# Where the modulation of two adaptive-norm layers is computed: TensorE in the mixers, or VectorE in the feed-forward blocks

## The chip, the cores and the metric

The kernel runs on one core of a Trainium2 chip. The metric is the device time of one execution in microseconds (us); the time before is the median of three runs. A profiled execution of the same kernel gives the rows below.

## The reference, cut to what matters

The program is one block of a first network (a feed-forward block "FFN1", a mixer of dilated attention and an RWKV recurrence, a feed-forward block "FFN2"), then two layers of a second network with two streams of 256 tokens each (`x` and `ctx`), width 1024. Each layer of the second network takes six vectors of width 1024 from a condition vector, for each stream:

```python
cond_x = silu(c); cond_c = silu(c_ctx)[None]
for layer in range(2):
    mod_x = split(cond_x @ w_mod[layer] + b_mod[layer], 6)      # w_mod[layer]: 1024 x 6144
    mod_c = split(cond_c @ w_mod[layer] + b_mod[layer], 6)
    hx = adaln(x, norm1_g, mod_x[0], mod_x[1]); hc = adaln(ctx, norm1_g, mod_c[0], mod_c[1])
    mix_x, mix_c = token_mixing(hx, hc, ...)                     # mix_c only in layer 0
    x = x + mod_x[2] * mix_x
    x = x + mod_x[5] * channel_mix(adaln(x, norm2_g, mod_x[3], mod_x[4]))   # layer 0: FFN, layer 1: 8 experts
    # ctx: the same, in layer 0 only
```

The modulation is thus two products of a matrix of 1024 x 6144 with two vectors. It depends on nothing but `c`, `c_ctx` and the weights. All numbers are float32.

## The kernel before, in words

The stages follow one another: FFN1 (`ffn_block`), the first mixer (`mix1`, with `attn1` and then `rwkv`), FFN2 (`ffn_block`), the mixer of layer 0 (`mix2(0)`), its feed-forward block for both streams (`ffn2_block`), the mixer of layer 1 (`mix2(1)`) and the experts (`moe`). Instructions are written as Python generators. A scheduler then sets a fixed order for each engine's queue; an instruction that is written earlier has the higher priority, and one whose inputs and buffers are free earlier may be placed before it. On the chip each queue is worked off in that order.

Weights come through `wraw` (L113): three buffers of 1 MB, loaded by SyncE's queue. `wsplit` (L137) turns each float32 weight tile into a high and a low part: ScalarE casts (`whi`, L149), VectorE subtracts (`wlo`, L150), into 8 pairs of buffers in FFN1 and FFN2 and 6 in `ffn2_block`. A product is then three matmuls (`mm3`, L160 to L162). In `ffn` (L253) the hidden width of 2816 is taken in two halves; a half has six steps over gate and up columns (L261 to L282), and then two column halves of the down product (L283 to L307). In each gate and up step VectorE also has `hh` and `hlo` (L277, L280).

The modulation is `mod` (L836). A column block of 512 of the 6144 columns takes two loads of 1 MB through `wraw` and eight matmuls (L844). Each has 32 columns of weights, two of which are the condition vectors, and writes one of four groups of 32 partitions of a PSUM tile; ScalarE copies the tile (L847), four transposes (L850) put the columns on partitions, and VectorE sums the four groups and adds the bias (L852, L853), into `modT`. After blocks 3 and 9 the gains `gsT` are made. The twelve blocks of layer 0 are woven into `rwkv` (L800: one step of `mod` after four of `rwkv`), with what is left of them behind it (L801). Blocks 0 to 5 of layer 1 are woven into the attention and mLSTM of `mix2(0)`, blocks 6 to 11 into those of `mix2(1)` (L958), and L962 takes what is left. In all, 24 blocks.

`cond` (L824) makes the columns `cT` of the condition vectors early in FFN1. `ffn2_block` makes the rows of its gates (`gate_rows`, 32 matmuls at L169) ahead of its `ffn` loop.

Of the kernel before, what the change touches and what calls it, by code (L numbers as in the profile page):

```python
# [9 lines left out]
F32 = mybir.dt.float32  # L10
# [3 lines left out]
OP = mybir.AluOpType  # L14
AX = mybir.AxisListType
# [4 lines left out]
KT = 8  # L20
# [9 lines left out]
def kview(w, r0, nk, c0, n):  # L30
    return w[r0:r0 + nk * 128, c0:c0 + n].rearrange("(k p) f -> p k f", p=128)


class Builder:
# [295 lines left out]
        nc.vector.scalar_tensor_tensor(y, y, rstd, grow, op0=OP.mult, op1=OP.mult)  # L330
        nc.vector.tensor_tensor(h, y, h, op=OP.add)

    def ffn_block(self, h, pre, wg, wu, wd, post, early=None):
        nc = self.nc
        with self.phase("fp", 8, gu=2, ps=6) as fp:
            x = self.norm_rows_T(fp, h, pre, 2)
            late = True
            for r in self.ffn([x], self.I[wg], self.I[wu], self.I[wd], fp):
                if late:
                    late = False  # L340
                    early()
                    grow = self.row(fp, post, 2)
                    y = self.row_tiles()
                if r is not None:
                    hf, c, t, p = r
                    yv = y[t][:, c * 512:(c + 1) * 512]
                    if hf == 0:
                        nc.scalar.copy(yv, p)
                    else:
                        nc.vector.tensor_tensor(yv, p, yv, op=OP.add)  # L350
                        if c == 1:
                            self.add_post(h[:, t], y[t], grow, 0.5)
                yield
# [482 lines left out]
    def mod(self, L, cbs=range(12), tag="md"):  # L836
        nc = self.nc
        w = self.I["w_mod_2"][L]
        for cb in cbs:
# [19 lines left out]
                                        .to_broadcast([128, KT, 2]), op=OP.mult)  # L859
            yield  # L860

    def ada_T(self, h, L, n, gi, tag="ps"):
        return self.norm_T(h, lambda k: self.gsT[:, L, n, k, gi:gi + 1],
                           lambda k: self.modT[:, L, 24 * n + k, gi:gi + 1], tag)
# [350 lines left out]
    def ffn2_block(self, early):  # L1215
        nc = self.nc
        with self.phase("fp", 6, gu=2, ps=6) as fp:
            xs = [self.ada_T(self.hx, 0, 1, 0), self.ada_T(self.hc, 0, 1, 1)]
            gr = [self.gate_rows(fp, 0, 40, g, "gr%d" % g) for g in range(2)]
            for r in self.ffn(xs, self.I["ffn_w1_2"], self.I["ffn_w3_2"], self.I["ffn_w2_2"], fp):  # L1220
                if r is not None:
                    hf, c, t, p = r
                    self.gated_add((self.hx, self.hc)[t // 2], t % 2, slice(c * 512, c * 512 + 512), p, gr[t // 2])
                    if (hf, c, t) == (1, 1, 3):
                        early()
                yield


# [308 lines left out]
def run(*gens):  # L1537
    for g in gens:
        for _ in g:
            pass  # L1540
# [78 lines left out]
def host_consts():  # L1619
    f = np.float32  # L1620
    out = {"k_ident": np.eye(128, dtype=f)}
    i = np.arange(128)
    t, s = i[:, None], i[None, :]
    same = (t // 64) == (s // 64)
    lm = np.zeros((128, 2, 2, 2, 64), f)
    lv = np.zeros((128, 7, 64), f)
    for d in range(2):
        before = (t < s) if d == 0 else (t > s)
        incl = before | (t == s)
        b, n = before[:64, :64], incl[:64, :64]  # L1630
        for c in range(2):
            lm[c * 64:c * 64 + 64, d, c] = np.stack([-b.astype(f), -n.astype(f)], 1)
            lm[64 - c * 64:128 - c * 64, d, c] = np.stack([b, n], 1)
    for li, m in enumerate((1, 2, 4, 8, 16, 32)):
        lv[:, li] = np.tile(((t // (2 * m) == s // (2 * m)) & (t // m != s // m))[:64, :64], (2, 1))
    lv[:, 6] = np.tile(np.eye(64), (2, 1))
    out["k_lm"] = lm
    out["k_lvl"] = lv
    out["k_blk"] = same.astype(f)
    q = np.arange(S)  # L1640
    diff = np.abs(q[:, None] - q[None, :])
    cnt = (diff <= 64).astype(np.int64) + (diff % 4 == 0) + (diff % 16 == 0)
    bias = np.where(cnt > 0, np.log(np.maximum(cnt, 1).astype(np.float64)), -1e30).astype(f)
    out["k_mask1"] = np.ascontiguousarray(bias.reshape(2, 128, S).transpose(1, 0, 2))
    pos = np.arange(S, dtype=f)
    inv = (f(10000.0) ** (-np.arange(0, 64, 2, dtype=f) / f(64))).astype(f)
    ang = (pos[:, None] * inv[None, :]).astype(f)
    c, sn = np.cos(ang).astype(f), np.sin(ang).astype(f)
    C = np.concatenate([c, c], 1)
    Sg = np.concatenate([-sn, sn], 1)  # L1650
    tab = np.stack([C / 8, Sg / 8, C, Sg], 1).astype(f)
    t4 = np.arange(S)
    iq = (f(10000.0) ** (-np.arange(16, dtype=f) / f(16))).astype(f)
    ar = ((t4 // 64).astype(f)[:, None] * iq[None]).astype(f)
    ac = ((t4 % 64).astype(f)[:, None] * iq[None]).astype(f)
    cr, sr, cc, sc = (np.cos(ar).astype(f), np.sin(ar).astype(f), np.cos(ac).astype(f), np.sin(ac).astype(f))
    C2 = np.concatenate([cr, cr, cc, cc], 1)
    S2 = np.concatenate([-sr, sr, -sc, sc], 1)
    tab2 = np.stack([C2 / 8, S2 / 8, C2, S2], 1).astype(f)
    out["k_rope2"] = np.ascontiguousarray(tab2.reshape(2, 128, 4, 64).transpose(1, 0, 2, 3))  # L1660
    ok = np.stack([t <= s, t >= s], 1)
    out["k_tri"] = ok.astype(f)
    out["k_trib"] = np.where(ok, 0.0, -1e30).astype(f)
    out["k_iota"] = np.ascontiguousarray(np.broadcast_to(np.arange(1, 257, dtype=f).reshape(2, 128), (128, 2, 128)))
    out["k_rope1"] = np.ascontiguousarray(tab.reshape(2, 128, 4, 64).transpose(1, 0, 2, 3))
    return out


def program(tc, I, out):
    b = Builder(tc, I)  # L1670
    b.out = out
    with ExitStack() as ctx:
        b.open_pools(ctx)
        b.consts()
        run(b.ffn_block(b.hx, "ffn1_pre_g", "ffn1_w_gate", "ffn1_w_up", "ffn1_w_down", "ffn1_post_g", b.cond))
        side = b.mod(0)
        run(b.mix1(side))
        run(side)
        pre = []

        def early():
            b.load_ctx()
            pre.append(b.ada_T(b.hc, 0, 0, 1))

        run(b.ffn_block(b.hx, "ffn2_pre_g", "ffn2_w_gate", "ffn2_w_up", "ffn2_w_down", "ffn2_post_g", early))
        run(b.mix2(0, b.mod(1, range(0, 6), "acc"), pre[0]))
        run(b.ffn2_block(lambda: pre.append(b.ada_T(b.hc, 1, 0, 1))))
        run(b.mix2(1, b.mod(1, range(6, 12), "acc"), pre[1]))
        run(b.moe())


# [6 lines left out]
def arrange(inputs):  # L1698
    out = {}
    for n in _RAW:  # L1700
        a = np.asarray(inputs[n])
        if n not in _WHOLE:
            a = a.reshape(a.shape[1:])
        if n in ("rwkv_w2", "rwkv_a2"):
            a = a.reshape(128, 512)
        if n == "w_router_2":
            a = a.reshape(KT, 128, 8).transpose(1, 0, 2)
        out[n] = np.ascontiguousarray(a)
    out["k_vec"] = pack_vec(vec_list(inputs))
    out.update(host_consts())  # L1710
    return out
# [16 lines left out]
```

## Time and profile before

| what | value |
|---|---|
| time before, median of three runs | 2446.23 us (2445.49 to 2446.34) |
| the profiled execution: its time, its span | 2445.14 us, 2443.4 us |
| TensorE busy | 2347.4 us, 96% |
| VectorE busy | 1613.0 us, 66% |
| ScalarE busy | 1308.8 us, 54% |
| granted TensorE clock, mean over the span | 0.987 |

The span runs from the first to the last instruction; the time has another 1.7 us around it. PE is TensorE's matmuls, PEld its weight loads, DVE VectorE, ACT ScalarE, POOL GpSimd, SPq SyncE's queue. An x and a number count instructions or records. Two records of L844 stand for one matmul. A matmul's length in the profile is modelled and overlaps the next one's, so that a busy TensorE is not always a full one; the time from one start to the next tells what it costs.

### The profile page before, as it was taken

The numbers are of one execution on the slowest core, as the hardware profiler recorded it, in microseconds if no ns is written. First come the engines' busy times: TensorE is split into PE (matmuls) and PEld (weight loads), VectorE is DVE, ScalarE is ACT, GpSimd is POOL, SyncE is SP. The second block draws the span as 40 slices with busy tenths as digits, with TensorE's granted clock in tenths as the row PEclk, the third lists the DMA queues.
The fourth block names the chain that finished last, engine by engine and source line by source line (L and its number), as shares of the span: only waits on it lengthen the run. The fifth ranks groups of instructions, "written<-read, shape, count | busy, mean of one in ns | idle before, by whom it ended". The sixth has DMA issues, their size and how long they took to land.

```text
span 2443.4 us, 38784 instructions
## 1 busy us (share of the span) xinstructions
PE 2347.4 (96%) x15592; PEld 1965.2 (80%) x15592; DVE 1613.0 (66%) x2425; ACT 1308.8 (54%) x2039; POOL 188.1 (8%) x248
## 2 busy tenths in 40 slices
PE   7998989979998999999999999989999999999997
PEld 7996866659998767799899886778888887887876
DVE  5555667647547466443333374669989989889897
ACT  5443644345535355433223253567887777777675
POOL 0001022110001000200100110020100110020000
PEclk9999999999999999999999999999999999999999
DMA  8654342275652350232332235369999999999994
GB/s 262 198 184 141 121 164 88 71 235 183 204 173 87 103 173 18 69 121 75 108 104 70 96 113 171 126 225 379 333 372 322 342 343 337 360 339 325 370 338 169
DMA packets 281117, 489.56 MB, mean 200 GB/s; under 512 B 11441, under 2 KB 116913, under 8 KB 280929
## 3 DMA queue, kind: packets, MB, share of 16 engines
q1 hardware_dynamic: 280848, 486.80, 58.3%
q8 instruction: 124, 2.03, 0.3%
q14 instruction: 65, 0.52, 0.1%
q0 software_dynamic: 80, 0.21, 0.0%
HBM read 485.92 MB, written 1.05 MB: 199 GB/s over the span
## 4 chain that ended last, share of the span: by engine, by line
PE 70%; issue 10%; DVE 6%; ACT 2%; POOL 1%; DMA 0%; POOLq 0%; DVEq 0%; ACTq 0%
PE gu L161 9%; PE gu L162 9%; PE gu L160 9%; PE acc L162 4%; PE acc L161 4%; PE acc L160 4%; PE dn L160 3%; PE dn L161 3%; PE dn L162 3%; DVE wlo L150 2%; PE ps L162 2%; PE ps L161 2%; PE ps L160 2%; PE acc L844 2%; PE ps L1079 2%
## 5 line engine op out<-in xcount | busy, mean ns | idle before, releaser
L150 DVE TENSOR_TENSOR wlo<-wraw,whi 128x1024 fp32r<-128x1024 f32 (+1 forms) x830 | 975.3, 1208 | 231.1 <-ACT whi L149 224.2
L149 ACT CAST whi<-wraw 128x1024 fp32r<-128x1024 f32 (+1 forms) x832 | 824.6, 1030 | 264.4 <-PE ps L162 102.3
L161 PE MATMUL gu<-xlo,whi 128*128 128x256 f32 x1408 | 394.5, 280 | 4.4 <-DVE xlo L193 2.7
L160 PE MATMUL gu<-xhi,whi 128*128 128x256 f32 x1408 | 394.5, 281 | 2.3 <-ACT xhi L192 1.5
L162 PE MATMUL gu<-xhi,wlo 128*128 128x256 f32 x1408 | 393.6, 280 | 0.0
L161 PE MATMUL gu<-wlo,X 128*128 128x512 f32 (+1 forms) x768 | 291.2, 379 | 4.4 <-DVE wlo L150 3.3
L162 PE MATMUL gu<-whi,X 128*128 128x512 f32 (+1 forms) x768 | 286.3, 373 | 0.0
L160 PE MATMUL gu<-whi,X 128*128 128x512 f32 (+1 forms) x768 | 285.0, 374 | 0.0
L161 PEld LDWEIGHTS gu<-xlo,whi 128*128 128x128 f32 x1408 | 264.7, 188 | 5.6 <-DVE xlo L193 3.2
L160 PEld LDWEIGHTS gu<-xhi,whi 128*128 128x128 f32 x1408 | 265.0, 189 | 3.7 <-ACT xhi L192 2.1
L162 PEld LDWEIGHTS gu<-xhi,wlo 128*128 128x128 f32 x1408 | 265.1, 188 | 0.0
L161 PEld LDWEIGHTS gu<-wlo,X 128*128 128x128 f32 x768 | 144.6, 188 | 45.5 <-DVE wlo L150 21.2
L160 PEld LDWEIGHTS gu<-whi,X 128*128 128x128 f32 x768 | 144.7, 188 | 25.5
L162 PEld LDWEIGHTS gu<-whi,X 128*128 128x128 f32 x768 | 144.7, 188 | 23.6
L161 PE MATMUL acc<-wlo,xhi 128*128 128x512 f32 (+1 forms) x368 | 142.6, 388 | 3.1 <-DVE wlo L150 3.0
L277 DVE TENSOR_TENSOR hh<-sg,gu 128x256 f32<-128x256 f32 x88 | 36.8, 418 | 164.7 <-ACT sg L275 164.7
L160 PE MATMUL acc<-whi,xhi 128*128 128x512 f32 (+1 forms) x368 | 141.7, 387 | 2.5 <-ACT whi L149 1.1
L162 PE MATMUL acc<-whi,xlo 128*128 128x512 f32 (+1 forms) x368 | 142.6, 388 | 0.1
L161 PE MATMUL dn<-wlo,hT 128*128 128x512 f32 x352 | 140.6, 399 | 0.0
L162 PE MATMUL dn<-whi,hT 128*128 128x512 f32 x352 | 138.6, 394 | 0.0
L160 PE MATMUL ps<-whi,hhi 128*128 128x512 f32 x352 | 137.1, 390 | 0.0
L162 PE MATMUL ps<-whi,hlo 128*128 128x512 f32 x352 | 137.1, 389 | 0.0
(469 smaller groups left out, 3742.5 us busy)
## 6 DMA issues: line engine op xcount, KB each, us to landing
wraw<-in_exp_w_dram SPq DMA_DIRECT2D x235, 1024.0 KB, 7.0
wraw<-in_w_mod_dram SPq DMA_DIRECT2D x48, 1024.0 KB, 5.2
wraw<-in_w_in_dram SPq DMA_DIRECT2D x29, 1024.0 KB, 5.2
wraw<-in_exp_w_dram SPq DMA_DIRECT2D x58, 512.0 KB, 6.5
wraw<-in_ffn_w_dram SPq DMA_DIRECT2D x28, 1024.0 KB, 5.4
wraw<-in_ffn_w_gate_dram SPq DMA_DIRECT2D x20, 1024.0 KB, 5.5
wraw<-in_ffn_w_up_dram SPq DMA_DIRECT2D x20, 1024.0 KB, 5.5
wraw<-in_ffn_w_down_dram SPq DMA_DIRECT2D x16, 1024.0 KB, 5.2
```

The source lines that it names most:

```text
L149: nc.scalar.copy(hi, raw[:, k0:k0 + n])
L150: eng.tensor_tensor(lo, raw[:, k0:k0 + n], hi.bitcast(F32), op=OP.subtract)
L160: mm(out, l[0], r[0], start=start, stop=False)
L161: mm(out, l[0], r[1], start=False, stop=False)
L162: mm(out, l[1], r[0], start=False, stop=stop)
L277: nc.vector.tensor_tensor(hh, sg, pg[:, 1], op=OP.mult)
L844: nc.tensor.matmul(p[32 * k:32 * k + 32], self.cT[:, 2 * (kb + k):2 * (kb + k) + 32], wt[:, k], start=kb == 0, stop=kb > 0)
L1079: nc.tensor.matmul(o[g, t][:, h], PT[:, kt], VA[:, k0 + kt, kv * 64:kv * 64 + 64], start=kt == 0, stop=kt == nk - 1)
```

## The change

A new function `mod_rows` computes the modulation on VectorE. For a column block it loads pieces of 512 KB (two row blocks of 128 rows, 512 columns) into tiles `mraw` of its own, and accumulates for each condition vector raw * c + acc, with 128 partitions by 512 columns to an instruction. After eight row blocks a 32x32 block transpose and a sum along the free axis bring 512 columns to 16 values on each partition. After a group of blocks one matmul with a constant `k_sel` sums over the partitions, and small additions on VectorE write `modT`.

It runs as a side generator inside the three feed-forward blocks: blocks 0 to 3 of layer 0 in FFN1, 4 to 7 in FFN2 (three `mraw` buffers, one step of two row blocks after each step of `ffn`), and in `ffn2_block` blocks 10 and 11 of layer 0 and all twelve of layer 1 (one `mraw` buffer, two steps after each step of `ffn`; blocks 4 to 11 of layer 1 for stream x alone). Blocks 8 and 9 of layer 0 stay with `mod` on TensorE, in `mix2(0)`. `rwkv` and `mix2(1)` have no modulation any more. In `ffn2_block` the gate rows move behind the sixth step.

```diff
-    def ffn_block(self, h, pre, wg, wu, wd, post, early=None):
+    def ffn_block(self, h, pre, wg, wu, wd, post, early, part):
...
                 if late:
                     late = False
-                    early()
+                    early(fp)
                     grow = self.row(fp, post, 2)
                     y = self.row_tiles()
+                    side = self.mod_rows(fp, 0, (part,), 3)
+                next(side, None)
...
+    def mod_rows(self, pool, L, parts, bufs=2):
+        nc = self.nc
+        w = self.I["w_mod_2"][L]
+        sel = self.load_const(pool, "k_sel", nc.sync)
+        for c0, c1, nv in parts:
+            R = pool.tile([128, c1 - c0, nv, 16], F32, name="mR", tag="mR%d" % c0)
+            for cb in range(c0, c1):
+                acc = pool.tile([128, 2, 512], F32, name="macc", bufs=1)
+                for k0 in range(0, KT, 2):
+                    raw = pool.tile([128, 2, 512], F32, name="mraw", bufs=bufs)
+                    nc.sync.dma_start(raw, kview(w, k0 * 128, 2, cb * 512, 512))
+                    for k in range(k0, k0 + 2):
+                        for v in range(nv):
+                            c = self.cT[:, 2 * k + v:2 * k + v + 1]
+                            if k == 0:
+                                nc.vector.tensor_scalar(acc[:, v], raw[:, k - k0], c, None, op0=OP.mult)
+                            else:
+                                nc.vector.scalar_tensor_tensor(acc[:, v], raw[:, k - k0], c, acc[:, v], op0=OP.mult, op1=OP.add)
+                    yield
+                for v in range(nv):
+                    tr = pool.tile([128, 16, 32], F32, name="mtr", bufs=1)
+                    nc.vector.transpose(tr.rearrange("p a b -> p (a b)"), acc[:, v])
+                    nc.vector.tensor_reduce(R[:, cb - c0, v], tr, axis=AX.X, op=OP.add)
+            n = c1 - c0
+            q = self.psum(n * nv * 16)
+            nc.tensor.matmul(q, sel, R.rearrange("p a b c -> p (a b c)"), start=True, stop=True)
...
+            for i in range(2):
+                if c0 <= 3 + 6 * i < c1:
+                    self.mod_gain(L, i, nv)
+            yield
...
     def ffn2_block(self, early):
...
-            gr = [self.gate_rows(fp, 0, 40, g, "gr%d" % g) for g in range(2)]
+            side, gr, i = self.mod_rows(fp, 0, ((10, 12, 2),), 1), None, 0
...
                     if (hf, c, t) == (1, 1, 3):
+                        run(side)
                         early()
+                i += 1
+                if i == 6:
+                    run(side)
+                    gr = [self.gate_rows(fp, 0, 40, g, "gr%d" % g) for g in range(2)]
+                    side = self.mod_rows(fp, 1, ((0, 4, 2), (4, 12, 1)), 1)
+                for _ in range(2):
+                    next(side, None)
                 yield
...
-        run(b.ffn_block(b.hx, ..., b.cond))
-        side = b.mod(0)
-        run(b.mix1(side))
-        run(side)
+        run(b.ffn_block(b.hx, ..., lambda p: b.cond(), (0, 4, 2)))
+        run(b.mix1(iter(())))
...
-        run(b.ffn_block(b.hx, ..., early))
-        run(b.mix2(0, b.mod(1, range(0, 6), "acc"), pre[0]))
+        run(b.ffn_block(b.hx, ..., early, (4, 8, 2)))
+        run(b.mix2(0, b.mod(0, range(8, 10), "acc"), pre[0]))
         run(b.ffn2_block(lambda: pre.append(b.ada_T(b.hc, 1, 0, 1))))
-        run(b.mix2(1, b.mod(1, range(6, 12), "acc"), pre[1]))
+        run(b.mix2(1, iter(()), pre[1]))
```

## Rows read from the trace of the kernel before

**Rows 1.** Busy time of each engine by stretch; then clock, DMA share, GB/s.

```profile
core 0: us, PE busy (x) PEld busy (x) DVE busy (x) ACT busy (x) POOL busy (x), PEclk, DMA share, GB/s
15.00:75.00 60.00, 58.18 (x479) 57.98 (x480) 36.79 (x48) 32.88 (x49) 0.00 (x0) 0.97 0.70 224
75.00:106.00 31.00, 31.00 (x163) 26.69 (x162) 17.12 (x18) 15.40 (x20) 0.00 (x0) 1.00 0.74 234
325.00:505.00 180.00, 169.09 (x2697) 113.72 (x2697) 121.58 (x329) 70.70 (x179) 32.38 (x42) 0.99 0.37 122
550.00:612.00 62.00, 60.59 (x506) 59.85 (x505) 44.13 (x65) 34.82 (x57) 1.88 (x4) 0.97 0.57 180
612.00:643.00 31.00, 31.00 (x163) 26.73 (x163) 17.14 (x18) 15.37 (x21) 0.00 (x0) 1.00 0.73 233
1055.00:1395.00 340.00, 340.00 (x2463) 322.00 (x2463) 121.62 (x166) 97.27 (x154) 20.26 (x15) 1.00 0.29 93
1605.00:2443.00 838.00, 813.88 (x3882) 666.39 (x3880) 739.82 (x752) 612.40 (x727) 57.89 (x39) 0.99 0.92 328
```

**Rows 2.** Chain that ended last: shares in 321.5 to 485 and 485 to 512.

```profile
by line: PE c L668 9.7%; PE md L844 8.9%; PE c L675 8.6%; PE c L628 4.9%; POOL Y L659 4.7%; DVE LM L631 4.2%; issue 3.3%; PE c L685 2.9%; DVE X L677 2.3%; PE c L696 2.0%; POOL mrs L111 1.9%; PE c L715 1.9%; DVE FT L670 1.8%; DVE cs L582 1.8
...
by line: PE md L844 44.1%; PE md L850 7.6%; PE c L675 6.4%; PE c L715 5.4%; PE c L685 5.4%; PE c L696 5.0%; PE c L704 4.6%; ACT mrow L847 4.4%; PE c L668 4.2%; PE c L718 3.8%; PE c L738 3.3%; PE c L719 2.6%; PE c L751 1.9%; DVE y L753 1.1%;
```

**Rows 3.** The same, in 837 to 905 (`mix2(0)`) and 1478 to 1555 (`mix2(1)`).

```profile
by line: PE acc L844 27.2%; PE ps L1079 10.9%; PE ml L1178 10.3%; PE at L1076 8.2%; PE ml L1149 7.6%; PE at L1056 7.5%; PE ml L1180 6.7%; PE ml L1162 5.3%; PE at L1055 4.7%; PE acc L850 4.0%; PE ml L1204 3.5%; PE ml L1133 1.5%; ACT mrow L84
...
by line: PE acc L844 25.4%; PE ps L1079 12.9%; PE at L1076 6.6%; PE ml L1204 5.5%; PE at L1056 5.5%; PE at L1055 5.3%; PE acc L162 4.5%; PE acc L161 4.5%; PE acc L160 4.5%; PE acc L850 4.0%; PE ml L1178 3.8%; PE ml L1180 3.8%; PE ml L1149 3
```

**Rows 4.** Pieces of the chain, in `rwkv` and `mix2(0)`: start, length, what.

```profile
486.30 0.99 PE md L844 x8
...
847.90 0.97 PE acc L844 x2
848.88 0.64 PE ml L1178 x4
849.52 0.99 PE acc L844 x6
```

**Rows 5.** VectorE's operations by line: count, shortest, median and longest in ns.

```profile
L979 DVE SCALAR_TENSOR_TENSOR om<-om,mg_r x6: 672/684/693, 938.0 to 1587.0; 128x512 f32<-128x512 f32 x6
...
L678 DVE STREAM_TRANSPOSE Y<-X x32: 402/438/446, 346.2 to 496.4; 128x256 f32<-128x256 f32 x32
...
L972 DVE TENSOR_REDUCE mg_s<-mg x6: 633/678/681, 895.0 to 1579.7; 128x4 f32<-128x512 f32 x6
```

**Rows 6.** VectorE in order of time: six scaled sums of 128x256 together.

```profile
775.88 2.46 DVE L1018 SCALAR_TENSOR_TENSOR cacc<-cpad,cvw,cacc 128x256 f32<-128x256 f32 x6
778.26 1.22 DVE L150 TENSOR_TENSOR wlo<-wraw,whi 128x1024 fp32r<-128x1024 f32 x1
```

**Rows 7.** Waits in 75 to 106: who for whom, us, times, longest.

```profile
DVE wlo L150 <- ACT whi L149: 10.1, 7, 2.9
ACT whi L149 <- PE ps L162: 8.8, 7, 3.0
```

**Rows 8.** Loads in 1055 to 1395: size, median us from issue to landing.

```profile
wraw<-in_ffn_w_dram SPq DMA_DIRECT2D x22, 1024.0 KB, 5.5
wraw<-in_ffn_w_dram SPq DMA_DIRECT2D x4, 768.0 KB, 4.8
wraw<-in_ffn_w_dram SPq DMA_DIRECT2D x4, 512.0 KB, 3.9
```

**Rows 9.** Chain pieces at the start of `ffn2_block`, and VectorE's waits in 1055 to 1395.

```profile
1035.70 1.53 PE ps L169 x6
1037.23 1.68 PE ps L243 x12
1039.84 2.03 PE ps L169 x16
...
DVE hh L277 <- ACT sg L275: 114.3, 31, 4.4
```

More of the change, by code (lines that the diff above doesn't have):

```diff
@@ L860, in mod @@
             yield
+    def mod_rows(self, pool, L, parts, bufs=2):
[24 more added lines that the diff above has]
+            nc.tensor.matmul(q, sel, R.rearrange("p a b c -> p (a b c)"), start=True, stop=True)
+            for c in range(4):
+                rs = slice(32 * c, 32 * c + 32)
+                qv = q[rs].rearrange("p (a v j c) -> p a v j c", v=nv, j=4, c=4)
+                for v in range(nv):
+                    nc.vector.tensor_tensor(self.modT[rs, L, 4 * c0:4 * c1, v].rearrange("p (a j) -> p a j", j=4), qv[:, :, v, :, c],
+                                            self.v("b_mod%d" % L, 4 * c0, 4 * n)[rs].rearrange("p (a j) -> p a j", j=4), op=OP.add)
+            for i in range(2):
+                if c0 <= 3 + 6 * i < c1:
+                    self.mod_gain(L, i, nv)
+            yield
@@ L862, in ada_T, with mod_gain @@
+    def mod_gain(self, L, n, nv=2):
+        nc = self.nc
+        gs = self.gsT[:, L, n, :, 0:nv]
+        nc.vector.tensor_scalar(gs, self.modT[:, L, 8 + 24 * n:16 + 24 * n, 0:nv], 1.0, None, op0=OP.add)
+        nc.vector.tensor_tensor(gs, gs, self.v("norm%d_g%d" % (n + 1, L), 0, KT)[:, :, None].to_broadcast([128, KT, nv]), op=OP.mult)
     def ada_T(self, h, L, n, gi, tag="ps"):
@@ L1639, in host_consts @@
     out["k_blk"] = same.astype(f)
+    out["k_sel"] = np.tile(np.eye(32), (4, 4)).astype(f)
     q = np.arange(S)
@@ L1674, in program, with early @@
         b.consts()
-        run(b.ffn_block(b.hx, "ffn1_pre_g", "ffn1_w_gate", "ffn1_w_up", "ffn1_w_down", "ffn1_post_g", b.cond))
-        side = b.mod(0)
-        run(b.mix1(side))
-        run(side)
+        run(b.ffn_block(b.hx, "ffn1_pre_g", "ffn1_w_gate", "ffn1_w_up", "ffn1_w_down", "ffn1_post_g", lambda p: b.cond(), (0, 4, 2)))
+        run(b.mix1(iter(())))
         pre = []
-        def early():
+        def early(p):
             b.load_ctx()
             pre.append(b.ada_T(b.hc, 0, 0, 1))
-        run(b.ffn_block(b.hx, "ffn2_pre_g", "ffn2_w_gate", "ffn2_w_up", "ffn2_w_down", "ffn2_post_g", early))
-        run(b.mix2(0, b.mod(1, range(0, 6), "acc"), pre[0]))
+        run(b.ffn_block(b.hx, "ffn2_pre_g", "ffn2_w_gate", "ffn2_w_up", "ffn2_w_down", "ffn2_post_g", early, (4, 8, 2)))
+        run(b.mix2(0, b.mod(0, range(8, 10), "acc"), pre[0]))
         run(b.ffn2_block(lambda: pre.append(b.ada_T(b.hc, 1, 0, 1))))
-        run(b.mix2(1, b.mod(1, range(6, 12), "acc"), pre[1]))
+        run(b.mix2(1, iter(()), pre[1]))
         run(b.moe())
```

## Prediction

> **What bounds the kernel now.** I read the busy time by stretch first. In FFN1, FFN2 and `ffn2_block` TensorE is busy nearly without a gap, while VectorE is busy 36.8 of 60 us and 17.1 of 31 us in FFN1, and 121.6 of 340 us in `ffn2_block` [rows 1]. So TensorE sets the time there and VectorE has room. In `rwkv` TensorE is busy 169 of 180 us and VectorE 121.6; in the experts the DMA engines are busy 92% and VectorE 88%, and nothing of this change reaches them [rows 1]. Then the chain that ended last says what the modulation costs where it stands. In `rwkv` L844 has 8.9% of the first 163.5 us, but L844, L850 and L847 have 44.1, 7.6 and 4.4% of the last 27 us: the modulation is late and empties at the end [rows 2]. In `mix2(0)` L844 and L850 have 31.2% of 68 us, in `mix2(1)` 29.4% of 77 us [rows 3]. The reader is to see that this work stands on the chain in all three mixers, although TensorE only multiplies by two vectors.
>
> **What leaves TensorE.**
>
> `rwkv`: the last stretch holds 27 x 56.1% = 15.1 us of modulation, the one before 163.5 x 8.9% = 14.6 us of L844 and, as L850 is below the last share shown, at most 1.8% or 2.9 us of it: at most 32.6 us. All of it comes back only if the recurrence's own steps are ready by then. In the last stretch TensorE alone carried the chain, so I take 13 of 15. Before it VectorE is at two thirds and GpSimd's and VectorE's steps (L659, L631) stand in the chain between the matmuls, so a part of L844 filled time that would pass anyway; I take half of some 16, or 8. Sum 21; bounds 10 (two thirds of the last stretch, nothing else) and 33.
>
> `mix2(0)`: 68 x 31.2% = 21.2 us for six blocks, 3.5 each. Two blocks are still done there, those of layer 0, so four leave: 14.1 us, of which I take 13. Bounds 8 and 14.
>
> `mix2(1)`: 77 x 29.4% = 22.6 us for six blocks; all leave. The output projection (L160 to L162, 13.5% of that stretch) and independent heads can move up into the gaps, so I take 20. Bounds 14 and 23.
>
> Together 54 us, between 32 and 70. The small operations on ScalarE and VectorE (L847, L852, L853) go with it, and the 2 MB of each block leave the three `wraw` buffers, so the output weights come earlier; I count nothing for that, since no wait for weights shows among the chain's shares [rows 2, 3].
>
> [...] Eight records of L844, four matmuls for the four column groups, take 0.99 us together at 486.30; at 847.90 one matmul alone takes 0.97, L1178 follows, and the other three take 0.99 [rows 4]. Split so, a half block costs twice as much. [...]
>
> **What VectorE takes on.** A scaled sum of 128x512 lasts 684 ns [rows 5]. Six of 128x256 take 2.46 us, and the next instruction starts 2.38 us after the first of them: 0.40 us from one to the next, and the last runs 0.08 us past that [rows 6]. Taking the same 0.08 off, I put 0.60 us for one of 512. A step of two row blocks and two vectors is four of these, 2.4 us. The sum over 512 elements is 0.68 us, the transpose of 256 is 0.44 [rows 5]; one of 512 lies between 0.44 and 0.88, and I take 0.65 with the overlap. So a block ends with 2 x (0.65 + 0.60) = 2.5 us, and costs 4 x 2.4 + 2.5 = 12.1 us for two vectors, 6 us for one. FFN1 and FFN2 get 48 us each, `ffn2_block` 6 x 12.1 + 8 x 6 = 121 us.
>
> FFN1: seventeen steps are tied to the first seventeen of 29 steps of `ffn`. Over the first half's gate and up part (60 us) VectorE's 36.8 becomes 36.8 + 6 x 2.4 + 1.5 x 2.5 = 55: it fits. Over the down part (31 us) it has 17.1 and gets ten steps: 17.1 + 24 + 6.3 = 47, 16 us too many. What covers this is the weights that are split ahead. There ScalarE's cast waits for TensorE to give buffers back, 8.8 us in 31 [rows 7], so all 8 pairs are full; they hold four loads, and as 31 us of TensorE use six, four cover 20 us. So 16 is just covered, and I take 2 us for order; 0 to 16.
>
> FFN2: in its first part VectorE is already at 44.1 of 62 us [rows 1], with 18 more at 62. The buffers are then not full when the down part starts; with half the cover, 10 us, 6 of the 16 are lost. I take 6; 0 to 18.
>
> `ffn2_block`: 121.6 + 121 = 243 of 340 us, 71%. Room, but one `mraw` buffer: a load can start only when the four sums before it are done, and lands 3.9 us after its issue [rows 8]. SyncE waits for that buffer with weight loads queued behind; those are 30 in 340 us [rows 8], 11 us apart, with three loads split ahead, so TensorE doesn't notice. The gate rows' 32 matmuls stood in the chain at the start (1.53 + 2.03 us shown) between transposes that waited for VectorE [rows 9]; now they stand inside full TensorE work. Nothing to 3.8 us, I take 2, and 2 more for the five `k_sel` matmuls that wait for VectorE. Together 4.
>
> Transfers: the down part of FFN1 moves 234 GB/s [rows 1]; 5 MB in 31 us more asks for 395, and 328 GB/s at a share of 0.92 [rows 1] bounds it near 356. That is 3.5 us late, inside the same 20 us of cover. Cost nothing; if the cover is gone, 3.5 us in each of the two.
>
> Sum: 2445.1 of the profiled execution - 54 + 12 = 2403.1; it ran 1.1 us under the median of the runs, so **2404 us**.
>
> **The rivals.**
>
> *All of it comes back* (chance 0.17). The chain's shares are then TensorE's true price and the cover holds: 2446 - 70 + 4 = 2380. For it: TensorE is busy 94% of `rwkv` [rows 1], and the chain in the two later mixers is nearly all TensorE's [rows 3]. Against: VectorE's and GpSimd's steps in the chain of `rwkv`.
>
> *The mixers have a second chain just behind* (0.16). Only the lower bounds return: 2446 - 32 + 12 = 2426. For it: behind the matmuls of `rwkv` stand L659, L631 and L677 on GpSimd and VectorE [rows 2].
>
> *VectorE bounds FFN1 and FFN2* (0.10). The cover is used up by the order in its queue; 16 + 18 + 9 us are lost: 2446 - 54 + 43 = 2435.
>
> *VectorE is held by landings in `ffn2_block`* (0.08, slower). Its queue has a fixed order. If the order expects the load earlier than it lands, VectorE stands at the first scaled sum, with `hh`, which frees the gate and up tiles, behind it. There are 9 + 48 steps and two group ends. Held for a full landing, that is 57 x 3.9 = 222 us, with 243 of work 465 in 340: 125 us too long, 2446 - 54 + 8 + 125 = 2525. From a hold of (340 - 243) / 57 = 1.7 us a step VectorE is the bound, and from 2.5 us the change loses. Against it: the wait for `hh`'s input is 114 us there [rows 9], time that the scheduler can fill with sums whose data have come.
>
> *The work on TensorE was hidden anyway* (0.04). No change, 2443 to 2449. The last 27 us of `rwkv` speak against it.
>
> **How the numbers follow.** The forecast has 0.45, with its own range of 2392 to 2414 (half of each doubt). Range for 8 in 10: from 2382, just above the case in which all returns, to 2435, the case of full VectorE in FFN1 and FFN2; outside are half of the first rival and the two last, about 0.2. A measurement of this kernel can tell about 0.2%, 5 us, from no change. Faster: 0.45 + 0.17 + 0.16 + 0.09 = 0.87; same 0.05; slower 0.08.
>
> **What the profile after would show.** Right: no L844 in `rwkv` and `mix2(1)`; `rwkv` ends about 20 us sooner after its start and `mix2(1)` 20; FFN1 lasts as before, FFN2 some 6 us longer, with TensorE waiting for `wlo` around the middle; scaled sums of 128x512 near 0.68 us, 0.60 apart; VectorE above 80% in the first halves of FFN1 and FFN2. Wrong: TensorE waiting for VectorE in many steps of `ffn2_block`, or VectorE's longest waits being for `mraw`; or a `rwkv` as long as before, with the chain on VectorE and GpSimd.

## The result and the profile after

| | before | after |
|---|---|---|
| median of 4 runs each | 2446.28 us (2445.49 to 2446.92) | 2471.88 us (2470.29 to 2474.74) |
| ratio, 95% interval | | 1.0103 (1.0091 to 1.0115) |
| the profiled execution: time, span | 2445.14, 2443.4 us | 2471.5, 2469.7 us |
| mean granted TensorE clock | 0.987 | 0.958 |
| TensorE busy, VectorE busy | 2347.4, 1613.0 us | 2304.5, 1829.6 us |

The change makes the kernel 25.6 us slower; the forecast was 42 us faster. TensorE is busy 43 us less and VectorE 217 us more. What went wrong is seen when the span is cut at the same events in both traces. A stage starts where the one before ends, and ends where the last addition of its results starts: L331 for FFN1, `mix1` and FFN2, the last `hc` addition on GpSimd for `mix2(0)`, the last `hx` addition for `ffn2_block` and for `mix2(1)`.

| us | FFN1 | `mix1` | FFN2 | `mix2(0)` | `ffn2_block` | `mix2(1)` | experts |
|---|---|---|---|---|---|---|---|
| before | 207.4 | 336.8 | 201.8 | 283.3 | 385.5 | 198.0 | 830.7 |
| after | 209.5 | 332.0 | 205.3 | 265.4 | 441.8 | 185.2 | 830.5 |
| difference | +2.1 | -4.8 | +3.5 | -17.9 | +56.3 | -12.8 | -0.2 |
| forecast | +2 | -21 | +6 | -13 | +4 | -20 | 0 |

Two entries hold nearly all of the error: `ffn2_block` costs 52 us more than the forecast, and `mix1` gives back 16 us less. The first is in the waits of the changed kernel from 1000 to 1460 us (who for whom, us in total, times, longest):

```profile
DVE macc L883 <- DMA mraw<-in_w_mod_dram: 103.0, 39, 5.9
...
PE ps L891 <- DVE mR L888: 40.4, 2, 31.3
```

TensorE, which before had no gap in 340 us of this block [rows 1], waits 40.4 us for two of the block's three `k_sel` matmuls (L891), and VectorE waits 103 us for landings of `mraw`. The order of time on TensorE at the longer of the two waits (start, length, what, idle before it):

```profile
1384.68 0.39 PE L161 MATMUL ps<-wlo,hhi 128*128 128x512 f32 x1
1384.90 0.39 PE L162 MATMUL ps<-whi,hlo 128*128 128x512 f32 x1
1416.55 0.80 PE L891 MATMUL ps<-mR,k_sel 128*128 128x128 f32 x2 [31.26 <-DVE mR L888]
1417.00 0.77 PE L160 MATMUL ps<-whi,hhi 128*128 128x512 f32 x1
1417.57 0.63 PE L161 MATMUL ps<-wlo,hhi 128*128 128x512 f32 x1
1418.00 0.63 PE L162 MATMUL ps<-whi,hlo 128*128 128x512 f32 x1
```

A matmul of 0.8 us stands in the queue between matmuls of the down product, which have their data, and holds them for 31 us. VectorE at the same time:

```profile
1397.16 0.75 DVE L883 SCALAR_TENSOR_TENSOR macc<-mraw,cT,macc 128x512 f32<-128x512 f32 x1
1402.85 1.54 DVE L883 SCALAR_TENSOR_TENSOR macc<-mraw,cT,macc 128x512 f32<-128x512 f32 x2 [4.94 <-DMA mraw<-in_w_mod_dram]
1408.13 1.54 DVE L883 SCALAR_TENSOR_TENSOR macc<-mraw,cT,macc 128x512 f32<-128x512 f32 x2 [3.73 <-DMA mraw<-in_w_mod_dram]
1413.49 1.54 DVE L883 SCALAR_TENSOR_TENSOR macc<-mraw,cT,macc 128x512 f32<-128x512 f32 x2 [3.83 <-DMA mraw<-in_w_mod_dram]
1415.06 0.71 DVE L887 STREAM_TRANSPOSE mtr<-macc 128x512 f32<-128x512 f32 x1
1415.81 0.69 DVE L888 TENSOR_REDUCE mR<-mtr 128x16 f32<-128x512 f32 x1
```

With one buffer a load starts only when the sums have read the one before. Load and sums take turns, 1.54 + 3.8 = 5.3 us a step, though VectorE has nothing else to do. The chain that ended last says the same for all of 1010 to 1455 us (the view cuts the line off):

```profile
by line: DMA mraw<-in_w_mod_dram 41.1%; DVE macc L883 18.6%; DVE wlo L150 5.7%; issue 5.5%; PE ps L162 2.5%; PE ps L160 2.5%; PE ps L161 2.5%; PE gu L161 2.3%; PE gu L160 2.2%; PE gu L162 2.2%; DVE post L922 1.6%; DVE macc L881 1.6%; DVE sp
```

Busy time by stretch, to set against [rows 1]; the sixth and seventh row are `ffn2_block` up to its long wait, and that wait:

```profile
core 0: us, PE busy (x) PEld busy (x) DVE busy (x) ACT busy (x) POOL busy (x), PEclk, DMA share, GB/s
15.00:75.00 60.00, 58.52 (x470) 58.22 (x471) 56.53 (x84) 31.36 (x49) 0.00 (x0) 1.00 0.95 314
75.00:106.00 31.00, 31.00 (x167) 26.83 (x167) 30.84 (x45) 14.22 (x19) 0.00 (x0) 1.00 0.83 275
325.00:505.00 180.00, 153.56 (x2498) 124.48 (x2498) 120.06 (x308) 68.56 (x174) 32.96 (x46) 0.81 0.02 5
550.00:612.00 62.00, 60.52 (x502) 60.23 (x503) 60.83 (x97) 32.44 (x54) 1.94 (x4) 0.96 0.76 239
612.00:643.00 31.00, 31.00 (x159) 26.53 (x159) 31.00 (x46) 12.85 (x18) 0.00 (x0) 1.00 0.85 274
1040.00:1380.00 340.00, 324.94 (x2389) 306.86 (x2388) 225.40 (x352) 91.68 (x152) 11.64 (x8) 0.98 0.51 161
1380.00:1420.00 40.00, 8.74 (x33) 6.92 (x32) 19.70 (x30) 1.56 (x2) 6.37 (x4) 0.60 0.39 119
```

In FFN1 and FFN2 VectorE is full or nearly so in both parts and TensorE stays busy: the weights split ahead do cover it. In `rwkv` (third row) there is no L844 left, and the granted clock is 0.81 where it was 0.99 [rows 1].

### The profile page after: what moved, and what is told of

Same layout as the page of the kernel before. It is cut to its first block, busy times and chain, and to the rows that moved or that the text cites. A ratio compares the mean times of both kernels' runs of the same rounds, so it can differ in the third digit from the quotient of the medians.

```text
span 2469.7 us, 38326 instructions
## 1 busy us (share of the span) xinstructions
PE 2304.5 (93%) x15162; PEld 1974.2 (80%) x15162; DVE 1829.6 (74%) x2777; ACT 1287.5 (52%) x2017; POOL 186.8 (8%) x248
## 4 chain that ended last, share of the span: by engine, by line
PE 58%; DVE 11%; issue 10%; DMA 8%; ACT 2%; POOL 1%; DVEq 0%; POOLq 0%; ACTq 0%
DMA mraw<-in_w_mod_dram 7%; PE gu L161 6%; PE gu L162 6%; PE gu L160 6%; PE acc L161 4%; PE acc L160 4%; PE acc L162 4%; DVE macc L883 3%; PE dn L160 3%; PE dn L162 3%; PE dn L161 3%; DVE wlo L150 3%; PE ps L1126 2%; PE at L1123 1%; ACT whi L149 1%
## 5 line engine op out<-in xcount | busy, mean ns | idle before, releaser
L883 DVE SCALAR_TENSOR_TENSOR macc<-mraw,cT,macc 128x512 f32<-128x512 f32 x252 | 180.4, 755 | 103.7 <-DMA mraw<-in_w_mod_dram 103.0
L161 PEld LDWEIGHTS gu<-wlo,X 128*128 128x128 f32 x768 | 144.7, 188 | 45.6 <-DVE wlo L150 21.2
L160 PEld LDWEIGHTS gu<-whi,X 128*128 128x128 f32 x768 | 144.8, 188 | 25.6
L162 PEld LDWEIGHTS gu<-whi,X 128*128 128x128 f32 x768 | 144.7, 188 | 23.6
```

Of the source, the lines that this page charges most:

```text
L160: mm(out, l[0], r[0], start=start, stop=False)
L161: mm(out, l[0], r[1], start=False, stop=False)
L162: mm(out, l[1], r[0], start=False, stop=stop)
L883: nc.vector.scalar_tensor_tensor(acc[:, v], raw[:, k - k0], c, acc[:, v], op0=OP.mult, op1=OP.add)
```

## The experiments

Single times are one execution; the kernel before took 2445.9 to 2448.8 us on the same chips. Two edits, `e2_late` and `e4_half_late`, moved nothing, since the steps that they moved had run out earlier: the order on every engine is that of the changed kernel and of `e1_half`. They serve as second runs of those. They also show how far a stage strays between two executions of one program: `mix1` took 332.0 us in the changed kernel and 338.4 in its second run, `ffn2_block` 441.8 and 436.0.

**Two half buffers.**

```diff
-                    raw = pool.tile([128, 2, 512], F32, name="mraw", bufs=bufs)
-                    nc.sync.dma_start(raw, kview(w, k0 * 128, 2, cb * 512, 512))
+                    if bufs > 1:
+                        raw = pool.tile([128, 2, 512], F32, name="mraw", bufs=bufs)
+                        nc.sync.dma_start(raw, kview(w, k0 * 128, 2, cb * 512, 512))
                     for k in range(k0, k0 + 2):
+                        if bufs == 1:
+                            one = pool.tile([128, 1, 512], F32, name="mraw", bufs=2)
+                            nc.sync.dma_start(one, kview(w, k * 128, 1, cb * 512, 512))
...
```

The sums, cut here, read `one[:, 0]` in place of `raw[:, k - k0]`.

> Edit: in ffn2_block the modulation loads pieces of one row block (256 KB) into two mraw buffers in turn, instead of 512 KB into one; same memory, same sums, same matmuls. Stage lengths of the changed kernel: FFN1 209, mix1 332, ffn2_block 441.8 us (385.5 before the change).
> Theory (one buffer makes load and sums take turns, 5.3 us a step at the end and more in the blocks with two vectors; the k_sel matmul then stands in TensorE's queue 31.3 and 9.1 us): with the next piece loading under the sums a step takes the longer of the two, some 4 us, 56 steps end about 95 us sooner, L891 waits less than 3 us each time, ffn2_block takes 398 to 406 us, the kernel 2427 to 2436.
> Rival (VectorE has no time left for the sums): the modulation ends within 20 us of where it does now, the wait stays above 20 us, the kernel 2455 to 2475.
> Third (the matmuls behind the wait were slow for another reason): the wait goes but less than 25 us comes back.

> Edit: the two of e1_half and e2_late together.
> Theory (one wait, two cures): since two buffers let the modulation end long before the place where its matmul stands, the place no longer matters: within 4 us of e1_half, 2426 to 2438 us.
> Rival (VectorE too full): two buffers leave a wait, and the later place takes it away: e4_half_late at least 8 us faster than e1_half.

Measured: 2442.05 and, as its second run, 2436.67 us, both above `e1_half`'s 2427 to 2436; `ffn2_block` 409.8 and 412.0 us. No wait for a `k_sel` matmul is left. In `e1_half` TensorE's longest waits from 1000 to 1480 us, and VectorE's longest, are

```profile
PE gu L160 <- DVE hh L277: 13.8, 8, 8.0
PE ps L243 <- DVE xn L215: 4.1, 4, 1.4
...
DVE macc L887 <- DMA mraw<-in_w_mod_dram: 65.1, 42, 4.4
```

So without the taking of turns there is no wait of 31 us. 24 to 27 of the 56 us remain, against the expected 13 to 20, and VectorE still waits 65.1 us for `mraw`. Over ten executions the mended change is no gain:

> The kernel of e1_half once more, timed in rounds: the change as made, with two half buffers instead of one in ffn2_block. Single times of it were 2442.05 and 2436.67 us. Theory (the loss against the kernel before was the one buffer's): faster than before, 2434 to 2444 us, ratio 0.995 to 0.999. Rival (the change does not pay even so): ratio 1.000 or more.

Measured: 2445.58 us median of ten (2443.92 to 2451.51), ratio 1.000 (0.9991 to 1.001); `ffn2_block` 413.2 us. The theory fell: the two single times, below all ten of these, had been lucky, and without the long wait the change is worth nothing.

**The place of the last `k_sel` matmul.**

> Edit: the last steps of the modulation, with their k_sel matmul, are issued after all matmuls of the down product instead of ahead of its last part; one buffer as in the changed kernel.
> Theory (a matmul that waits for VectorE holds all that is queued behind it on TensorE): the 31.3 us wait goes, since the down product runs under the modulation's last steps; the 9.1 us wait stays; ffn2_block takes 406 to 414 us, the kernel 2436 to 2446.
> Rival (the down product or the start of mix2(1) needs VectorE itself, which is behind): the wait shows up again at the end of the down product or at the start of mix2(1), and the kernel takes 2462 to 2475.

Measured 2471.79 us, the same order and the same time as the changed kernel, so this theory was not put to the test. The edit that does it, `e6_hold`, takes the last step out of the loop:

```diff
-                    side = self.mod_rows(fp, 1, ((0, 4, 2), (4, 12, 1)), 1)
+                    rest = self.mod_rows(fp, 1, ((0, 4, 2), (4, 12, 1)), 1)
+                    side = zip(range(49), rest)
...
                 yield
+            run(rest)
```

> Edit: the very last step of layer 1's modulation (last transposes and reductions, k_sel matmul, adds) is issued behind the whole loop of ffn2_block, one buffer as in the changed kernel. e2_late, meant to do this, issued the same order as the changed kernel, since the steps had run out before the place that it moved; it counts as a second run of it.
> Theory A (the k_sel matmul in TensorE's queue is the cause of the 31.3 us): the wait goes and the kernel takes 2438 to 2448.
> Theory B (the matmul is only the first to show that VectorE is some 30 us behind; the last weights' wlo stand behind the same sums in VectorE's queue): the wait moves to another line that VectorE feeds, 20 us or more of it, and the kernel takes 2460 to 2474.

Measured 2447.74 us, `ffn2_block` 413.1: of the block 23 to 29 us come back, of the kernel 24. The long wait is gone and the first, 9.1 us in the changed kernel, stays; what takes the long one's place is 3.6 us:

```profile
PE ps L891 <- DVE mR L888: 8.9, 1, 8.9
...
PE ps L161 <- DVE wlo L150: 3.6, 1, 3.6
```

Theory A holds. VectorE is as late as before: its last scaled sum starts 402 us after the block's start in both kernels. But TensorE lacks split weights for only 3.6 us, so nearly all of the long wait was the matmul's place in the queue.

**Two loads instead of 56.**

```diff
+        one = None
...
-                    raw = pool.tile([128, 2, 512], F32, name="mraw", bufs=bufs)
-                    nc.sync.dma_start(raw, kview(w, k0 * 128, 2, cb * 512, 512))
+                    if bufs > 1 or one is None:
+                        raw = one = pool.tile([128, 2, 512], F32, name="mraw", bufs=bufs)
+                        nc.sync.dma_start(raw, kview(w, k0 * 128, 2, cb * 512, 512))
```

> Edit: in ffn2_block only the first 512 KB piece of each modulation call is loaded and all its sums read that piece, so that the sums, transposes and matmuls stay and the other loads go (what layer 1's modulation holds is then not the reference's). ffn2_block took 385.5 us before the change, 441.8 in the changed kernel, 409.8 and 412.0 with two half buffers (e1_half and its twin e4_half_late).
> Theory (the rest of the loss, 25 us behind two half buffers, is VectorE standing at landings with the FFN's own hh, hlo and wlo queued behind: 65 us of waits for mraw): ffn2_block takes 386 to 396 us, TensorE's waits for hh go below 3 us, the kernel 2414 to 2426.
> Rival (the sums' own 120 us on VectorE crowd out the FFN's work): 404 to 414 us, as with two half buffers, the kernel 2432 to 2442.

Measured 2431.91 us, `ffn2_block` 399.2: the block is between the two forecasts, the kernel at the rival's edge. Of what half buffers left (409.8 to 413.2 us), 11 to 14 us were landings (one execution, of a block that strays by some 6 us between two); the 14 us that remain against the kernel before stand with the loads gone, so they are the sums themselves and what goes with them. TensorE's longest wait there, and three stretches in the columns above, show how:

```profile
PE gu L160 <- DVE hh L277: 5.6, 1, 5.6
...
1070.00:1090.00 20.00, 20.00 (x172) 20.00 (x171) 20.00 (x34) 6.68 (x11) 0.00 (x0) 1.00 0.43 133
...
1210.00:1230.00 20.00, 18.46 (x128) 17.05 (x126) 18.54 (x21) 2.46 (x4) 7.38 (x4) 1.00 0.30 95
1230.00:1250.00 20.00, 15.89 (x121) 15.89 (x122) 16.09 (x24) 6.41 (x11) 0.00 (x0) 0.83 0.27 81
```

Two steps to each step of `ffn` fill VectorE from 1050 to 1210 us (19.4 to 20.0 us of each 20); TensorE pays when the next half's gate and up part needs `hh`, 5.6 us in one wait, and then runs at a lower clock, 0.83 in 1230 to 1250 us.

**Fill in the recurrence without loads.**

```diff
+    def keep(self, n, tag="md"):
+        for _ in range(n):
+            p = self.psum(512, tag=tag)
+            for k in range(4):
+                self.nc.tensor.matmul(p[32 * k:32 * k + 32], self.cT[:, 2 * k:2 * k + 32], self.hx[:, k // 2, k % 2 * 512:k % 2 * 512 + 512], start=True, stop=True)
+            yield
...
-        run(b.mix1(iter(())))
+        run(b.mix1(b.keep(23)))
```

> Edit: 23 side steps of four column-group matmuls (the shape of the modulation's, on tiles that lie in memory, no load, nobody reads the result) are woven into the recurrence of mix1; they add work of some 23 us to TensorE.
> Theory (without the fill TensorE's granted clock falls to 0.5 to 0.9 in 330 to 510 us, and the recurrence's own matmuls take the longer): the clock is back at 0.94 or more there, the recurrence ends some 22 us sooner as it did before the change, and mix1 takes 310 to 320 us instead of 332.0; the kernel 2450 to 2460.
> Rival (the recurrence waits for VectorE and ScalarE, and the clock hardly matters): the added work lands on its path or under its waits, mix1 takes 330 to 356 us, the kernel 2470 to 2495.

> Edit: as e3_keep with 36 steps of four column-group matmuls on resident tiles instead of 23, as many as the modulation's steps before the change; no loads, nobody reads the result. Milestones of mix1, counted from the end of FFN1, are the four starts of the reciprocal roots of the recurrence's parts on GpSimd (mrs): 182.3, 224.2, 262.6, 308.9 us before the change; 185.7, 229.3, 270.5, 313.4 in the changed kernel; 184.6, 224.2, 268.5, 313.4 with 23 steps.
> Theory (the recurrence is a chain through VectorE and ScalarE with TensorE's pauses in it; fill lies in the pauses and holds the clock up): milestones three and four come at 262 to 266 and 308 to 311, the clock stays at 0.94 or more up to the recurrence's end, mix1 takes 326 to 330 us.
> Rival (added work lands on the path once the clock is up): fourth milestone at 315 or later, mix1 334 us or more.

Measured: 2466.67 us with 23 steps, 2467.84 with 36. The four `mrs` milestones and the end of `mix1`, in us from the end of FFN1 (`e7_swap` and `e9_swap_two` follow below):

| | 1 | 2 | 3 | 4 | end | 4 to end |
|---|---|---|---|---|---|---|
| before | 182.3 | 224.2 | 262.6 | 308.9 | 336.8 | 27.9 |
| after | 185.7 | 229.3 | 270.5 | 313.4 | 332.0 | 18.6 |
| its second run | 185.7 | 228.7 | 275.4 | 319.8 | 338.4 | 18.6 |
| 23 steps | 184.6 | 224.2 | 268.5 | 313.4 | 332.0 | 18.6 |
| 36 steps | 183.2 | 222.7 | 267.5 | 311.2 | 329.8 | 18.6 |
| `e7_swap` | 184.4 | 227.1 | 265.5 | 310.9 | 339.8 | 28.9 |
| `e9_swap_two` | 189.1 | 245.2 | 289.5 | 338.0 | 356.7 | 18.7 |

All seven executions here that have no fill in `mix1` (the changed kernel, its second run and five of the runs on `ffn2_block`) took 332.0 to 338.4 us for it, with the fourth milestone at 313.4 to 319.8.

With 23 steps `mix1` lasts as long as the shortest of these: the theory's 310 to 320 us did not come. The stage is in the rival's range, at its short end, so that the added work came under waits and not on the path; the kernel's time is between the two forecasts. The fill had run out before the recurrence ended:

```profile
480.00:500.00 20.00, 15.23 (x246) 13.13 (x244) 6.83 (x18) 2.06 (x7) 0.00 (x0) 0.59 0.01 2
```

With 36 steps, some 36 us of matmuls more than none, it is 329.8 us, as the theory had it; the third and fourth milestones miss its ranges by 1.5 and 0.2 us. That is 2 us under the shortest without fill, less than a stage strays. So the fill costs nothing here. The 20 us with the lowest clock in the changed kernel, then the same stretch with 36 steps:

```profile
340.00:360.00 20.00, 16.27 (x170) 13.02 (x169) 13.61 (x29) 7.25 (x18) 6.48 (x8) 0.50 0.00 1
```

```profile
340.00:360.00 20.00, 18.27 (x287) 10.62 (x283) 16.36 (x40) 6.91 (x16) 5.84 (x8) 1.00 0.01 2
```

Without fill TensorE still shows 16 of 20 us busy, but at half the clock and with 170 records instead of 287, of which 40 are fill: busy time is no measure here of what it does. The chain of the recurrence has VectorE's and GpSimd's steps between its matmuls (in the changed kernel `Y` on GpSimd has 4.5% and `X` on VectorE 3.0% of the chain that ended last from 325 to 505 us); fill stands in those pauses, and the clock is 1.00 in every such stretch from 340 to 520 us.

**The two layers exchanged.** Layer 0 back on TensorE in `mix1`, layer 1 on VectorE, nothing left in the later mixers:

```diff
-                    side = self.mod_rows(fp, 0, (part,), 3)
+                    side = self.mod_rows(fp, 1, (part,), 3)
...
-            side, gr, i = self.mod_rows(fp, 0, ((10, 12, 2),), 1), None, 0
+            gr = [self.gate_rows(fp, 0, 40, g, "gr%d" % g) for g in range(2)]
+            side = self.mod_rows(fp, 1, ((8, 12, 1),), 1)
...
-                for _ in range(2):
-                    next(side, None)
+                next(side, None)
...
-        run(b.mix1(iter(())))
+        side = b.mod(0)
+        run(b.mix1(side))
+        run(side)
...
-        run(b.ffn_block(b.hx, "ffn2_pre_g", "ffn2_w_gate", "ffn2_w_up", "ffn2_w_down", "ffn2_post_g", early, (4, 8, 2)))
-        run(b.mix2(0, b.mod(0, range(8, 10), "acc"), pre[0]))
+        run(b.ffn_block(b.hx, "ffn2_pre_g", "ffn2_w_gate", "ffn2_w_up", "ffn2_w_down", "ffn2_post_g", early, (4, 8, 1)))
+        run(b.mix2(0, iter(()), pre[0]))
```

> Edit: layer 0's twelve column blocks go back to TensorE inside the recurrence of mix1, as before the change; VectorE sums layer 1's instead: blocks 0 to 3 (two vectors) in FFN1, 4 to 7 (one vector) in FFN2, 8 to 11 (one vector, 16 steps, one buffer) in ffn2_block; mix2(0) and mix2(1) have no modulation left.
> Theory (a stage pays by what it hides: the recurrence hid its fill nearly whole, since the change won 4.8 us there and e3_keep put 23 steps back for nothing, while mix2(0) and mix2(1) paid 18 and 13 us; and ffn2_block loses by 56 waits for landings, not by 16): FFN1 209, mix1 335 to 338, FFN2 203 to 205, mix2(0) 260 to 265, ffn2_block 387 to 397, mix2(1) 181 to 186, the kernel 2408 to 2424, faster than both.
> Rival (work of the same kind costs the same wherever it stands, and the recurrence's 21 us are lost again): 2435 or more.

Measured: 2411.17 us median of four (2406.68 to 2416.27), ratio 0.985 (0.9834 to 0.9867): faster than both kernels, and each stage within 2 us of its forecast (the two rows below it are runs that follow):

| us | FFN1 | `mix1` | FFN2 | `mix2(0)` | `ffn2_block` | `mix2(1)` | experts |
|---|---|---|---|---|---|---|---|
| before | 207.4 | 336.8 | 201.8 | 283.3 | 385.5 | 198.0 | 830.7 |
| `e7_swap` | 207.1 | 339.8 | 202.0 | 259.7 | 390.6 | 184.7 | 830.6 |
| `e9_swap_two` | 210.2 | 356.7 | 199.8 | 259.8 | 389.5 | 183.2 | 830.1 |
| `e10_swap_keep` | 209.1 | 338.5 | 201.8 | 258.1 | 393.7 | 204.0 | 831.5 |

The same one `mraw` buffer now costs 5 us in `ffn2_block`, since there are 16 steps of two sums each instead of 56 with two or four, one after each step of `ffn`, and its `k_sel` matmul does not wait; VectorE's waits for landings there:

```profile
DVE macc L883 <- DMA mraw<-in_w_mod_dram: 20.0, 9, 4.7
```

**Ending the fill sooner.** The change gave `mix1` 4.8 us, and the milestones put them behind the recurrence. SyncE's queue there in `e7_swap` (start, length, what), then in the changed kernel:

```profile
442.19 61.72 SPq L133 DMA_DIRECT2D wraw<-in_w_mod_dram  x9
504.00 0.46 SPq L177 DMA_DIRECT2D grow<-in_mix_post_g_dram  x1
507.11 19.43 SPq L133 DMA_DIRECT2D wraw<-in_w_out_dram  x8
```

```profile
477.75 0.33 SPq L177 DMA_DIRECT2D grow<-in_mix_post_g_dram  x1
506.35 11.01 SPq L133 DMA_DIRECT2D wraw<-in_w_out_dram  x5
```

With the modulation's loads ahead of them all eight loads of `w_out` come late; without, three have landed earlier, ahead of the recurrence, and five are left.

```diff
-                    yield from weave(self.rwkv(mp, me, R, yT), side, 4)
+                    yield from weave(self.rwkv(mp, me, R, yT), side, 2)
```

> Edit: as e7_swap, and the modulation's steps in mix1 are woven in after every second step of the recurrence instead of every fourth, so that they and their loads end sooner.
> Theory (the 4.8 us that mix1 gave back came behind the recurrence: its loads of w_out follow the modulation's loads in SyncE's queue and its three buffers; from the fourth mrs milestone to the end of mix1 it takes 27.9 us before the change and 28.9 in e7_swap, 18.6 in the changed kernel and in e8_keep36, which has the fill without its loads): the stretch behind the milestone falls to 19 to 22 us, the milestone stays within 4 us, mix1 takes 328 to 333 us instead of 336.8 (before) or 339.8 (e7_swap), the kernel 2400 to 2408.
> Rival (a denser fill no longer fits into the chain's pauses): the milestone comes 6 us or more later, nothing is won, the kernel 2408 to 2420.

Measured: 2431.37 us, ratio 0.9943 (0.9926 to 0.996), 20 us slower than `e7_swap`. Both came true at once: the stretch behind milestone 4 fell to 18.7 us, and the milestone came 27 us later. Three of the eight loads now go early:

```profile
326.53 141.54 SPq L133 DMA_DIRECT2D wraw<-in_w_mod_dram  x21
471.79 10.22 SPq L133 DMA_DIRECT2D wraw<-in_w_out_dram  x3
```

The rival decides. Fill cost nothing at one step after every fourth of the recurrence; woven twice as densely it delays the chain, by 27 us at the milestone, and the pauses at the end stay empty. None of TensorE's waits there ends with a landing, so that it is not the loads' landings that hold it. What the stretch behind the milestone waited for is less clear: in `e7_swap` the modulation's own work ends late too (ScalarE copies its last tile at 513.99 us and casts the first piece of `w_out` at 514.47), and in `e9_swap_two` loads and matmuls both end sooner. Which of them sets the 9 us is not separated.

**Fill in `mix2(1)` without loads.** As `e7_swap`, with 18 steps of `keep` (on `hc`, tag "acc") as the side work of `mix2(1)`:

> Edit: as e7_swap, and 18 side steps of four column-group matmuls on resident tiles, without loads and read by nobody, are woven into mix2(1), where the kernel before had 18 steps of modulation with their loads. mix2(1) took 198.0 us before the change, 184 to 185 without modulation.
> Theory (here TensorE itself is the limit, 97% busy before, so that added matmuls land on the path): mix2(1) takes 193 to 200 us.
> Rival (the loads were what cost, as in mix1: those of w_in and w_out behind the modulation's): 184 to 188 us.

Measured 2438.84 us; `mix2(1)` 204.0 us, above even the theory's 193 to 200 and 19.3 more than in `e7_swap`, or 1.07 us for each step of four matmuls, which take 0.99 together [rows 4]. There the matmuls themselves cost, not their loads. It is the opposite of `mix1`, with instructions of the same shape. The six blocks of the kernel before have 12 such groups of four and not 18: 12 x 1.07 = 12.8 us, an estimate beside the 13.3 that `e7_swap` gains there.

## Why the prediction was wrong

The sum had the right terms, and two of them failed by far.

**`ffn2_block`, "and 2 more for the five `k_sel` matmuls that wait for VectorE".** This is the step that turned the sign: 40.4 us instead of 2, for two of the three `k_sel` matmuls of this block (five is their number in the whole kernel). Right before it stood "Room, but one `mraw` buffer: a load can start only when the four sums before it are done, and lands 3.9 us after its issue", and the consequence was not worked out. From the prediction's own numbers, 24 steps with four sums take 24 x (3.9 + 2.4) = 151 us, 32 with two 32 x (3.9 + 1.2) = 163, and 20 transposes and reductions 20 x 1.25 = 25: 339 of 340 us, for a chain behind whose last matmul 37 us of the block's work were still queued (1416.55 to 1454.0). "71%" of VectorE was the wrong question; a chain of load and sums in turn has its own length, and VectorE's share says nothing of it. `e1_half` takes the turns away and `e6_hold` the place in the queue; each alone removes the 31 us.

**The rival that ended slower** had the right place and the wrong form. It priced VectorE standing at landings with `hh` behind it, 125 us and a chance of 0.08. VectorE did stand there, 103 us, but mostly in time it had to spare: the part that `e5_one_load` can put down to landings beyond the long wait is 11 to 14 us, and the sums' crowding 14. These two, some 25 us, are in the forecast at nothing. The list of signs named the right view, "VectorE's longest waits being for `mraw`".

**`rwkv`, "so I take 13 of 15" and half of the rest, 21 us.** Of this nothing came from the recurrence: its milestone 4 lies at 313.4 to 319.8 us without fill and at 308.9 to 313.4 with it at the density of before, and the 4.8 us stand behind it. As I read it, the chain's shares of L844 and L850 [rows 2] are the time that TensorE spent on fill while the next step was also on its way; a share of the chain is what ended last, not what returns. The rival "hidden anyway" was right for this stage alone. The argument against it, the last 27 us, fell: `e8_keep36` puts the matmuls back there and the stage is no longer.

**"I count nothing for that"**, the output weights that come earlier. In `mix1` all of the gain stands in the stretch that waits for them, 27.9 - 18.6 = 9.3 us, less the 4.5 to 11 us by which the recurrence is slower without fill. The reason given, "no wait for weights shows among the chain's shares", rests on rows that end at 512 us; in the kernel before these loads run on to 523.5:

```profile
504.49 19.05 SPq L133 DMA_DIRECT2D wraw<-in_w_out_dram  x8
```

**Terms of the right kind.** `mix2(1)`: 12.8 (13.3 in `e7_swap`) against 20, under its bounds; of shares of 22.6 us some 13 return, 2.2 us a block, and `e10_swap_keep` shows that it is the matmuls' price. `mix2(0)`: 17.9 against 13, above its bounds; all six blocks give 23.6 in `e7_swap`, 3.9 each, where the shares [rows 3] came to 21.2. So the work does stand on the path in both, but the size of its share told the gain in one of them alone; what gives a block 1.7 us more in `mix2(0)` was not tested. FFN1 +2.1 against 2 and FFN2 +3.5 against 6: the cover of split weights holds although VectorE is full. VectorE's own work was priced too low, 141 us in `ffn2_block` (L881, L883, L887, L888) instead of 121: scaled sums start 0.66 us apart in the blocks with two vectors and 0.79 in those with one, where each sum reads what the last one wrote, and 0.60 was worked out; transposes take 0.71 and reductions 0.69 us where 0.65 and 0.60 were taken. Four sums of a step with two vectors in the changed kernel, three starts and one length of 0.75 together:

```profile
1085.12 2.74 DVE L883 SCALAR_TENSOR_TENSOR macc<-mraw,cT,macc 128x512 f32<-128x512 f32 x4 [2.55 <-DMA mraw<-in_w_mod_dram]
```

**What stays open.** How long the recurrence would be without fill and with the clock at 1.00 was not tried, since in these runs the clock was at 1.00 all through 340 to 520 us with 36 steps of fill, and at 0.50 to 0.98 without; so how much of the free fill is pauses and how much is the clock it returns is not separated. Nor is what sets the 9.3 us behind the recurrence, the late loads of `w_out` or the modulation's own late end.

## What to carry to other kernels

Work out the length of each chain that takes turns with itself (one buffer: landing plus use, times the steps) before asking whether an engine has time, and look for what stands in the other engines' queues at its end. Before moving work off an engine, ask whether its stage pays for it: the same matmuls cost 1.07 us a step in `mix2(1)` and nothing in the recurrence, and the two layers exchanged made 1.0103 into 0.985. The density of fill matters as much as its amount: after every fourth step of the recurrence it cost nothing here, after every second 20 us of the kernel.

## What the runs showed of the hardware

Taking work from TensorE lowered its clock here. In the recurrence the granted clock of 340 to 360 us is 1.00 in the kernel before, 0.50 in the changed kernel without fill, and 1.00 with 36 steps of fill. Before the fall TensorE worked with short pauses (the longest 2.9 us) and no fill: the clock is 1.00 in 320 to 325 us, 0.68 in 325 to 330, where TensorE is busy 2.10 of 5 us, and 0.50 from 330 to 360, although TensorE shows 16.27 us busy in the 20 from 340 on. With 36 steps of fill it is 0.91 in 320 to 340 us and 1.00 in each 20 us from there to 520. In `ffn2_block` it is 0.60 in the 40 us with the long wait, in which TensorE is busy 8.74 us, and the first matmuls behind it run 0.43 us apart, the down product's usual pitch being 0.23. The runs do not show how much of a pause lowers the clock, nor what brings it back: in the changed kernel it is 0.98 again in 360 to 380 us, without fill.

Two half buffers took away a part of the waits for landings: VectorE waits 65.1 us for `mraw` in `e1_half` instead of 103.0 with one buffer, in the same memory.
